# One decoder layer on one core: constant matmuls at the start, row scales by diagonals, two weight blocks kept, sums in two steps and on GpSimd, gmlp output stored whole

## The chip, the cores and the metric

The kernel runs on one core of one Trainium2 chip. The metric is the device time of one execution in microseconds (us), lower is better. Before the change it is 1546.96 us, the median of three runs (1548.9, 1546.96 and 1545.43). The engines are named as in the profile: PE (matmuls; PEld is its weight load), DVE (vector), ACT (scalar), POOL (GpSimd) and SP, whose queue issues most of the DMAs.

## The reference

One layer of a hybrid decoder on a prompt of 1024 tokens and on 64 sample tokens (8 sequences of 8) that share the weights; D = 1024, fp32 inputs.

```python
h = rmsnorm(x, norm_mix)
q, k, v, gu, gv, ga, gb = split_in(h @ w_in)     # 1024, 256, 256, 768, 768, 1024, 1024 columns
o, nk, nv = attn_prompt(q, k, v, sinks)          # window 128; the samples use a cache
vn = layernorm(jax.nn.gelu(gv), ln_g, ln_b)
s = spatial_gating(jax.nn.gelu(gu), vn, ws, bs)  # u * (W_s LN(v) + b) in chunks of 128
merged = jax.nn.sigmoid(ga) * (o @ w_pa) + jax.nn.sigmoid(gb) * (s @ w_pb)
x = x + merged @ w_out
f, nconv = conv_ffn(rmsnorm(x, norm_ffn), w_up, conv_w, conv_b, w_down, conv_prev)
return x + f, ...
```

`rmsnorm` is x / sqrt(mean(x²) + eps) times a gain. What the change touches is `h = rmsnorm(x, norm_mix)`, the product `h @ w_in`, and the way s gets from `spatial_gating` to `s @ w_pb`.

## The kernel before

**Precision.** Every operand of a matmul is split into a high part, which is the value rounded to fp32r, and a low part, which is the rest (`split`, L39 to L41: the ACT cast is L40, the DVE subtraction L41). One product then takes three matmuls: high·high, high·low, low·high.

**Groups and stages.** The tokens are in two groups: group 0 has 576 (64 samples and four blocks of 128), group 1 has 512 (four blocks of 128). The stages follow one another on PE, and what follows is about the first three:

- *Tokens* (to about 112 us). v has 256 columns, gv has three blocks of 256. The tokens are the stationary operand, the weights move (matmul line L489). A block of 256 weight columns is two items of 512 KB, each loaded to `wraw` and split into `w2h` and `w2l` (128x8x128 each time); there are two buffers of each. The order is v, gv0, gv1, gv2 for group 0 and the same again for group 1, so every block is loaded and split twice. v and gv come out as rows of tokens, so their scale 1/rms is one number for each partition (`rstg`).
- *Pairs* (about 112 to 475 us). q, k, gu and the two gates come out transposed. Here the weights are stationary (matmul line L288), and two weight tiles of 128 columns are taken together as a pair in a Strassen-Winograd scheme with seven products, `Chain.product`. It needs sums of the four quarters of a pair's weights (`Weights.total`, L173, four sums of 128x512 to `ws`, two buffers) and sums of the activations (`combine`, L250 to L253: two subtractions on POOL, then two steps on DVE that use them). A sum or a quarter is then split to `wh` and `wl`. The list of pairs begins with three *single* pairs that are done for group 0 only (FEWA = 3), then come 13 for both groups, then three singles for group 1 only.
- *Attention and branch* (from about 475 us) reads s and the queries back.

**The row scales.** `stats(g)` gets the sum of squares of the rows (`rs`, made by L562 on DVE), and from it 1/rms twice: one number for each partition by matmuls with a column of ones (L462), and as a full 128-row copy for the transposed activations, by matmuls of ones with `rs` (L467), two square roots on ACT and a reciprocal of the whole tile on DVE (L469). The jobs `t0_job` and `t1_job`, one for each step of the tokens stage, scale x by it (L603), call `combine`, and split the result for group 0 (`T0h`) or write it out for group 1 (`t1d`). It is read back and split (`t1_split`) during the first singles.

**Queues.** SP issues its DMAs in the program's order: weight items, x, the stores of gv (L521) and of the pairs' results. The weight stream is `Weights.get(ahead, loads)`: with each product it makes sure that the next operands are split and that `loads` more items are on their way, in a ring of four raw buffers. Each engine works its instructions in order, so an instruction that waits holds back those behind it.

**The gmlp output.** `mix_job` makes s for one channel group, splits it into high and low, and stores both planes (L743). `load_s` (L785) reads both planes back in the last singles and in the attention stage, straight to where PE uses them.

## Time and profile before

| what | value |
|---|---|
| runs | 1548.9, 1546.96, 1545.43 us, median 1546.96 |
| the profiled execution | 1547.57 us |
| span of its instructions | 1545.9 us (1.67 us of the execution lie around it) |
| mean granted PE clock | 0.993 |
| HBM read, written | 203.36 MB, 94.26 MB |
| DMA rate over the span | 193 GB/s |

The windows used below give for a stretch of time how long each engine was busy, with the number of its instructions in brackets, the granted PE clock as a share of full speed (PEclk), the busy share of the DMA engines and their rate. PE's busy time counts a matmul that runs at half clock as busy, so idle time and clock are read together.

### The profile page before, as it was taken

The page shows a single profiled execution, that of the slowest core. Times are in us where ns is not written, and L with a number is a line of the kernel's source. Part 1 is how long each engine was busy: PE and PEld are TensorE (multiplying, and loading weights), DVE is VectorE, ACT ScalarE, POOL GpSimd, SP SyncE. Part 2 cuts the span into 40 slices and gives each one's busy share as a digit, 9 for nine tenths or more (in the row PEclk, how much of TensorE's full clock was granted, in tenths as well). Part 3 has the DMA queues.
Part 4 walks back from the last instruction along what each step waited for, and adds up shares of the span by engine and source line. Part 5 has one row for each costly group of instructions (what it writes and reads, how often), then busy time and mean ns, then how long its engine had stood idle before and what let it go on. Part 6 is the DMA issues. An engine that isn't in the chain of part 4 may idle for free.

```text
span 1545.9 us, 30252 instructions
## 1 busy us (share of the span) xinstructions
PE 1518.0 (98%) x11588; PEld 1470.5 (95%) x11588; DVE 1182.7 (77%) x1908; ACT 863.9 (56%) x1800; POOL 274.4 (18%) x390
## 2 busy tenths in 40 slices
PE   8998999999999999999999999999999999999997
PEld 8998999999998888997988999999999999999997
DVE  6688776686664686888767888898899888785685
ACT  6656676765454574774443555555555556353462
POOL 0021000111020121230134222232232222000003
PEclk9999999999999999999999999999999999999999
DMA  6678344667779645828987423332233226973453
GB/s 230 226 259 297 136 161 177 223 193 244 262 271 325 230 164 179 265 81 300 329 304 265 159 90 112 120 125 99 101 141 114 79 93 219 360 246 94 122 176 131
DMA packets 134688, 297.63 MB, mean 193 GB/s; under 512 B 15504, under 2 KB 35792, under 8 KB 134544
## 3 DMA queue, kind: packets, MB, share of 16 engines
q1 hardware_dynamic: 134400, 295.69, 55.9%
q8 instruction: 91, 1.49, 0.4%
q14 instruction: 53, 0.43, 0.1%
q10 hardware_dynamic: 144, 0.01, 0.0%
HBM read 203.36 MB, written 94.26 MB: 193 GB/s over the span
## 4 chain that ended last, share of the span: by engine, by line
PE 78%; DVE 5%; DMA 3%; ACT 3%; issue 2%; POOL 1%; SPq 0%; POOLq 0%; ACTq 0%; DVEq 0%
PE st L288 45%; PE mm L234 15%; PE dn L1545 13%; PE po L1116 1%; PE sc L1068 1%; DMA sd<-sx 1%; DMA wraw<-wt 1%; PE pt L1095 1%; DVE wl L41 1%; ACT s L1085 1%; DVE ws L173 0%; DVE tl L41 0%; ACT wh L40 0%; DVE sx L41 0%; DVE s L1088 0%
## 5 line engine op out<-in xcount | busy, mean ns | idle before, releaser
L288 PE MATMUL st<-th,wh 128*128 128x256 f32 (+1 forms) x2128 | 613.9, 288 | 10.3 <-ACT ku L269 4.3
L288 PE MATMUL st<-tl,wh 128*128 128x256 f32 (+1 forms) x2128 | 610.9, 287 | 0.0
L288 PE MATMUL st<-th,wl 128*128 128x256 f32 (+1 forms) x2128 | 610.2, 287 | 0.0
L288 PEld LDWEIGHTS st<-th,wh 128*128 128x128 f32 x2128 | 402.3, 189 | 13.7 <-ACT k L269 6.1
L288 PEld LDWEIGHTS st<-th,wl 128*128 128x128 f32 x2128 | 402.6, 189 | 0.0
L288 PEld LDWEIGHTS st<-tl,wh 128*128 128x128 f32 x2128 | 402.2, 189 | 0.0
L40 ACT CAST wh<-wraw 128x512 fp32r<-128x512 f32 (+2 forms) x210 | 143.1, 692 | 105.0 <-PE mm L234 35.9
L41 DVE TENSOR_TENSOR wl<-wraw,wh 128x512 fp32r<-128x512 f32 (+2 forms) x210 | 163.0, 788 | 27.9 <-ACT wh L40 25.5
L1545 PE MATMUL dn<-tl,wh 128*128 128x288 f32 (+1 forms) x616 | 178.1, 289 | 0.2 <-DVE tl L41 0.2
L1545 PE MATMUL dn<-th,wh 128*128 128x288 f32 (+1 forms) x616 | 178.1, 289 | 0.0
L1545 PE MATMUL dn<-th,wl 128*128 128x288 f32 (+1 forms) x616 | 176.4, 286 | 0.0
L40 ACT CAST wh<-ws 128x512 fp32r<-128x512 f32 x168 | 103.0, 623 | 100.1 <-PE st L288 57.2
L41 DVE TENSOR_TENSOR wl<-ws,wh 128x512 fp32r<-128x512 f32 x168 | 116.4, 706 | 37.7 <-ACT wh L40 36.2
L1545 PEld LDWEIGHTS dn<-th,wh 128*128 128x128 f32 x616 | 116.9, 190 | 0.0
L1545 PEld LDWEIGHTS dn<-tl,wh 128*128 128x128 f32 x616 | 115.5, 187 | 0.5 <-DVE tl L41 0.5
L1545 PEld LDWEIGHTS dn<-th,wl 128*128 128x128 f32 x616 | 115.6, 188 | 0.0
L489 PE MATMUL st<-w2h,hh 128*128 128x256 f32 x288 | 82.5, 287 | 5.1 <-ACT w2h L40 5.1
L40 ACT CAST th<-traw 128x544 fp32r<-128x544 f32 (+1 forms) x85 | 54.4, 642 | 58.7 <-PE dn L1545 36.0
L276 POOL TENSOR_TENSOR z<-kn,k 128x288 f32<-128x288 f32 (+1 forms) x32 | 31.7, 995 | 289.6 <-ACT kn L271 286.0
L489 PE MATMUL st<-w2l,hh 128*128 128x256 f32 x288 | 82.0, 285 | 1.0 <-DVE w2l L41 1.0
L489 PE MATMUL st<-w2h,hl 128*128 128x256 f32 x288 | 81.7, 284 | 0.0
L41 DVE TENSOR_TENSOR tl<-traw,th 128x544 fp32r<-128x544 f32 (+1 forms) x85 | 61.5, 727 | 26.3 <-ACT th L40 26.1
(263 smaller groups left out, 2956.1 us busy)
## 6 DMA issues: line engine op xcount, KB each, us to landing
wraw<-wt SPq DMA_DIRECT2D x141, 512.0 KB
traw<-td SPq DMA_DIRECT2D x77, 272.0 KB
td<-za SPq DMA_DIRECT2D x22, 544.0 KB
wraw<-wt SPq DMA_DIRECT2D x35, 256.0 KB
upd<-hl SPq DMA_DIRECT2D x14, 512.0 KB
td<-t SPq DMA_DIRECT2D x11, 544.0 KB
qd<-q SPq DMA_DIRECT2D x8, 576.0 KB
q<-qd SPq DMA_DIRECT2D x8, 576.0 KB
```

What stands on the lines that cost most here:

```text
L40: S.copy(hi, src)
L41: V.tensor_sub(lo, src, hi.bitcast(F32))
L234: PE.matmul(ps[:, lo:lo + c1 - c0], u[:, k, :], v[:, c0:c1], start=(k == 0 and i == 0), stop=(k == nk - 1 and i == 2))
L276: op(to, pick(x, to, lo, hi), pick(y, to, lo, hi))
L288: PE.matmul(ps, u[:, kk, :], v, start=first and kk + i == 0, stop=kk == 3 and i == 2, skip_group_check=True)
L489: PE.matmul(ps, u[:, lo:lo + P], v[:, k, :], start=k + i == 0, stop=k == KD - 1 and i == 2)
L1068: PE.matmul(ps[:, h, o0:256], q, kst[kv][:, e, k0:cur + P], start=e == 0, stop=e == 1)
L1085: S.activation(s[:, h], s[:, h], AF.Exp, bias=nm[:, h:h + 1], accum_out=dn[:, h:h + 1])
L1095: PE.transpose(pt[:, h * P:h * P + P], s[:, h, 0:P], ident)
L1116: PE.matmul(po, v[:, kv, :], t, start=e == 0, stop=e == len(parts) - 1)
L1545: PE.matmul(place(m, e), u[:, m, :], v[:, lo:hi], start=new and i + k == 0 and (e == 0 or m % 2 == 0), stop=i == NU - 1 and k == 2, skip_g ...
```

## The change

1. **Constant matmuls.** Eight matmuls of a 128x128 tile of ones with itself are issued on PE ahead of the first real ones.
2. **Row scales by diagonals.** The full copy of 1/rms is made out of the one number for each partition: DVE multiplies the identity by it (a diagonal for each block of tokens), PE multiplies ones by the diagonal, ACT copies the result to `rs`. This is a job (`rows`) in the next block of the tokens stage. The matmuls of ones with `rs`, the four square roots on them and the two reciprocals of 576 and 512 columns are gone.
3. **Two blocks kept.** The order for group 0 is gv0, gv1, v, gv2. Group 1 then begins with v and gv2, whose weights still lie in the two buffers, and takes gv0 and gv1, loaded and split again. Four items of 512 KB, four casts and four subtractions are gone. The group's first steps have other jobs beside them than before.
4. **Sums in two steps.** `first_sums` scales x and issues the two POOL subtractions one job ahead of `sums_of`, which does the two DVE steps on them.
5. **Stores of gv** are issued from ACT's queue, and no longer from SP's.
6. **Single pairs.** The weight sums of the first pairs (14 sums of 128x512) are POOL's; the others stay on DVE. In most singles the last products of a pair load two items ahead, not one. The jobs that split T1 leave out every fourth product.
7. **gmlp unsplit.** s is stored as one plane, and read back to a stage buffer and split there (12 casts and 12 subtractions, in the last singles and ahead of the attention stage, where before there were 12 splits in the pairs stage).

The diff, cut to the lines that change:

```diff
         self.loaded = self.emitted = self.used = 0
-        self.sm = None
+        self.sm, self.adds = None, V
...
             t = self.sm.tile([P, 4, P], F32, name="ws", bufs=2)
-            V.tensor_add(t, x, y)
+            self.adds.tensor_add(t, x, y)
...
 t1d = [dr(f"t1d{kk}", [P, 7, 256]) for kk in range(4)]
-sd_ = [[dr(f"sd{g}{c}", [P, 2, n]) for c in range(NG)] for g, n in ((0, 576), (1, 512))]
+sd_ = [[dr(f"sd{g}{c}", [P, n]) for c in range(NG)] for g, n in ((0, 576), (1, 512))]
...
-    def dest256(key, half):
+    def dest256(key, half, again=False):
...
         def ready():
-            return "pool" in wide
+            return "pool" in wide and ("again" in wide or not again)
...
-    for g in range(2):
-        for i in range(2):
-            W.add(wt(V0 + i), KD, dest256(("v", g), i))
-        for i in range(6):
-            W.add(wt(GV0 + i), KD, dest256(("gv", g, i // 2), i % 2))
+    blocks = {"gv0": GV0, "gv1": GV0 + 2, "gv2": GV0 + 4, "v": V0}
+    for key in ("gv0", "gv1", "v", "gv2"), ("gv0", "gv1"):
+        for x in key:
+            for i in range(2):
+                W.add(wt(blocks[x] + i), KD, dest256(x, i, len(key) == 2))
...
-        acc, n2 = rsg[g], groups[g]["n"] // 2
+        acc, n = rsg[g], groups[g]["n"]
...
         V.reciprocal(rstg[g], rstg[g])
-        for h in range(2):
-            s, ps = slice(n2 * h, n2 * h + n2), bank()[:, :n2]
-            PE.matmul(ps, ones, acc[:, s], start=True, stop=True)
-            S.activation(acc[:, s], ps, AF.Sqrt, bias=eps, scale=1.0 / D)
-        V.reciprocal(acc, acc)
...
+        dg = stage(n)
+        for i, (name, lo) in enumerate(groups[g]["toks"]):
+            m = NS if name == "s" else P
+            V.tensor_scalar(dg[0:m, lo:lo + m], ident[0:m, 0:m], rstg[g][0:m, i:i + 1], None, ALU.mult)
...
+        def rows():
+            ps, at = None, 512
+            for name, lo in groups[g]["toks"]:
+                m = NS if name == "s" else P
+                if at + m > 512:
+                    ps, at, lo0 = bank(), 0, lo
+                PE.matmul(ps[:, at:at + m], ones[0:m], dg[0:m, lo:lo + m], start=True, stop=True)
+                at += m
+                if at + P > 512 or lo + m == n:
+                    S.copy(acc[:, lo0:lo + m], ps[:, :at])
+        return rows
...
         S.activation(v, ps, AF.Gelu_apprx_tanh, scale=rstg[g][:, i:i + 1])
-        nc.sync.dma_start(gvd[groups[g]["toks"][i][0]][:, 256 * p3:256 * p3 + 256], v)
...
-    def tokens(g, key, out, jobs):
-        W.get()
-        W.get()
+        nc.scalar.dma_start(gvd[groups[g]["toks"][i][0]][:, 256 * p3:256 * p3 + 256], v)
...
+    def tokens(g, key, out, jobs, new=True):
+        if new:
+            W.get()
+            W.get()
...
     xk = [hp0.tile([P, 576], F32, name=f"x{k}") for k in range(KD)]
-    places = [dest256(("v", 0), i)[1]() for i in range(2)]
+    places = [dest256("gv0", i)[1]() for i in range(2)]
...
             nc.sync.dma_start(xk[0][:, 320:576], a["xt"][0:P, 320:576])
+    ps = bank()
+    for _ in range(8):
+        PE.matmul(ps[:, 0:P], ones, ones, start=True, stop=True)
...
             for i, (_, lo) in enumerate(toks0):
-                mm_tok(ps5[i], 0, lo, wide["v", 0], kx)
+                mm_tok(ps5[i], 0, lo, wide["gv0"], kx)
...
         load_late()
-    stats(0)
+    rows = stats(0)
...
     for i in range(len(toks0)):
-        v_out(0, i, ps5[i])
+        gv_out(0, i, 0, ps5[i])
...
-    jobs = [x_job(k) for k in range(KD)]
-    for p3 in range(3):
-        tokens(0, ("gv", 0, p3), lambda i, ps: gv_out(0, i, p3, ps), jobs)
+    jobs = [rows, *(x_job(k) for k in range(KD))]
+    tokens(0, "gv1", lambda i, ps: gv_out(0, i, 1, ps), jobs)
+    tokens(0, "v", lambda i, ps: v_out(0, i, ps), jobs)
+    tokens(0, "gv2", lambda i, ps: gv_out(0, i, 2, ps), jobs)
...
     hs0o.close()
-    stats(1)
+    rows = stats(1)
...
+    half = {}
...
+    def first_sums(n):
+        def go():
+            g, kk = n // 4, n % 4
+            x_in(n + 1)
+            n2, x = groups[g]["n"] // 2, xin.pop(n)
+            for e in range(2):
+                k = kk + 4 * e
+                V.scalar_tensor_tensor(x[:, e], x[:, e], gains[:, 0, k:k + 1], rsg[g], ALU.mult, ALU.mult)
+            t4 = xr.tile([P, 4, 288], F32, name="t", bufs=2)[:, :, :n2]
+            b11, b12, b21, b22 = (x[:, e, n2 * h:n2 * h + n2] for e in range(2) for h in range(2))
+            G.tensor_sub(t4[:, 2], b22, b12)
+            G.tensor_sub(t4[:, 0], b11, b12)
+            half[n] = x, t4, b11, b21
+        return go
...
     def sums_of(g, kk):
-        x_in(4 * g + kk + 1)
-        n2, x = groups[g]["n"] // 2, xin.pop(4 * g + kk)
-        for e in range(2):
-            k = kk + 4 * e
-            V.scalar_tensor_tensor(x[:, e], x[:, e], gains[:, 0, k:k + 1], rsg[g], ALU.mult, ALU.mult)
-        t4 = xr.tile([P, 4, 288], F32, name="t", bufs=2)[:, :, :n2]
-        combine(t4, *(x[:, e, n2 * h:n2 * h + n2] for e in range(2) for h in range(2)))
-        return x[:, 0, 0:n2], t4, x[:, 1].rearrange("p (h c) -> p h c", h=2)
+        x, t4, b11, b21 = half.pop(4 * g + kk)
+        V.scalar_tensor_tensor(t4[:, 1], t4[:, 2], -1.0, b11, ALU.mult, ALU.subtract)
+        V.scalar_tensor_tensor(t4[:, 3], t4[:, 1], -1.0, b21, ALU.mult, ALU.subtract)
+        return b11, t4, x[:, 1].rearrange("p (h c) -> p h c", h=2)
...
     none = lambda: None
-    jobs = [lambda: x_in(0)] + [x for kk in range(4) for x in (t0_job(kk), none)] + [t1_job(kk) for kk in range(4)]
-    tokens(1, ("v", 1), lambda i, ps: v_out(1, i, ps), jobs)
-    for p3 in range(3):
-        tokens(1, ("gv", 1, p3), lambda i, ps: gv_out(1, i, p3, ps), jobs)
...
+    def both(*gos):
+        return lambda: [go() for go in gos]
...
+    jobs = [both(rows, lambda: x_in(0)), first_sums(0)]
+    for n in range(4):
+        jobs += [both(t0_job(n), first_sums(n + 1))] + [none] * (n % 2 == 0)
+    jobs += [both(t1_job(n), first_sums(n + 5)) for n in range(3)] + [t1_job(3)]
+    tokens(1, "v", lambda i, ps: v_out(1, i, ps), jobs, False)
+    wide["again"] = True
+    W.emit(W.used + 2)
+    tokens(1, "gv2", lambda i, ps: gv_out(1, i, 2, ps), jobs, False)
+    for p3 in range(2):
+        tokens(1, f"gv{p3}", lambda i, ps: gv_out(1, i, p3, ps), jobs)
...
             V.tensor_mul(t[:, soff:n], t[:, soff:n], gu[:, soff:n])
-            sx = mp.tile([P, 2, 576], F32R, name="sx")[:, :, :n]
-            split(sx[:, 0], sx[:, 1], t)
-            nc.sync.dma_start(sd_[g][c], sx.bitcast(F32))
+            nc.sync.dma_start(sd_[g][c], t)
...
     def load_s(g, pool, c):
-        x = pool.tile([P, 2, groups[g]["n"]], F32R, name=f"s{g}{c}")
-        nc.sync.dma_start(x.bitcast(F32), sd_[g][c])
+        n = groups[g]["n"]
+        raw, x = stage(n), pool.tile([P, 2, n], F32R, name=f"s{g}{c}")
+        nc.sync.dma_start(raw, sd_[g][c])
+        split(x[:, 0], x[:, 1], raw)
...
         for j in range(7):
-            w = W.get(3, 4 if at == len(seq) - 1 and j > 3 else 1)
+            W.adds = G if at < FEWA else V
+            single = at < FEWA - 1 or at >= len(seq) - FEWA - 1
+            w = W.get(3, 4 if at == len(seq) - 1 and j > 3 else 2 if single and j > 4 else 1)
...
                 done.pop(0)()
-            if jobs and 7 * at + j > 2:
+            if jobs and 7 * at + j > 2 and (at >= FEWA or (7 * at + j) % 4 < 3):
...
```

What it moves, first on POOL, from the last subtractions for group 0 to the first products of the pairs. `t` are the activations' sums, `ws` the weights' sums, `z` the pairs' results. Before:

```order
L251 TENSOR_TENSOR t_1563<-x_1517 128x256
L250 TENSOR_TENSOR t_1604<-x_1558 128x256
L251 TENSOR_TENSOR t_1604<-x_1558 128x256
L250 TENSOR_TENSOR t_1654<-x_1599 128x256
L251 TENSOR_TENSOR t_1654<-x_1599 128x256
L276 TENSOR_TENSOR z10_1771<-kn_1875,k5_1820 128x288
```

After:

```order
L173 TENSOR_TENSOR ws_1804<-wraw_1464,wraw_1466 128x512
L628 TENSOR_TENSOR t_1549<-x_1503 128x256
L627 TENSOR_TENSOR t_1549<-x_1503 128x256
L173 TENSOR_TENSOR ws_1881<-wraw_1625 128x512
L173 TENSOR_TENSOR ws_1903<-ws_1881,wraw_1623 128x512
L628 TENSOR_TENSOR t_1587<-x_1544 128x256
L627 TENSOR_TENSOR t_1587<-x_1544 128x256
L173 TENSOR_TENSOR ws_1928<-ws_1903,wraw_1623 128x512
L173 TENSOR_TENSOR ws_1951<-wraw_1623,wraw_1625 128x512
L173 TENSOR_TENSOR ws_2038<-wraw_1629 128x512
L276 TENSOR_TENSOR z10_1772<-kn_1870,k5_1821 128x288
```

Between the subtractions for group 1 now stand sums of weights: in all, six of the 14 stand ahead of the last of these subtractions, eight behind it.

On DVE at the first statistics (`rst` is the number for each partition, `rs` the full copy, `vst` and `gv` the outputs of the first block). Before:

```order
L562 TENSOR_TENSOR rs_231<-rs_231,x_257 128x576
L562 TENSOR_TENSOR rs_231<-rs_231,x_258 128x576
L376 COPY_PREDICATED c_wss<-stg 64x384
L464 RECIPROCAL rst_233<-rst_233 128x5
L41 TENSOR_TENSOR w2l<-wraw,w2h 128x8x128
L469 RECIPROCAL rs_231<-rs_231 128x576
L41 TENSOR_TENSOR vst<-gv,vst 128x4x64 x2
L507 TENSOR_TENSOR gv<-gv 128x256
```

After:

```order
L578 TENSOR_TENSOR rs_231<-rs_231,x_257 128x576
L578 TENSOR_TENSOR rs_231<-rs_231,x_258 128x576
L41 TENSOR_TENSOR w2l<-wraw,w2h 128x8x128
L376 COPY_PREDICATED c_wss<-stg 64x384
L464 RECIPROCAL rst_233<-rst_233 128x5
L469 TENSOR_SCALAR stg<-c_ident,rst_233 64x64
L469 TENSOR_SCALAR stg<-c_ident,rst_233 128x128 x4
L41 TENSOR_TENSOR w2l<-wraw,w2h 128x8x128
L45 SCALAR_TENSOR_TENSOR hl_608<-stg,c_gains,hh_607 128x512
L624 SCALAR_TENSOR_TENSOR x<-x,c_gains,rs_231 128x576
```

The reciprocal of 576 columns is gone, and five products with the identity stand in its place; the vst splits follow later, since the first block is now gv0.

On SP's queue in the last singles (`sd` is the stored s, `wraw` the raw weights of the last pairs). Before:

```order
L801 DMA msamp<-msamp 128x384
L814 DMA ckt<-ckt 128x1024
L785 DMA s_6016<-sd_175 128x1152
L785 DMA s_6038<-sd_176 128x1152
L144 DMA wraw<-wt 128x1024
L778 DMA sg0d_129<-z_5885 128x512
```

After:

```order
L824 DMA stg<-sd_175 128x576
L144 DMA wraw<-wt 128x1024
L781 DMA sd_186<-stg 128x512
L816 DMA sg0d_136<-z_5560 128x576
L816 DMA sg0d_136<-z_5562 128x512
L816 DMA sg1d_144<-z_5563 128x512
L841 DMA kn<-ksn 128x128
L841 DMA vs<-vsd 64x256
L841 DMA msamp<-msamp 128x384
L816 DMA sg1d_144<-z_5561 128x576
L854 DMA ckt<-ckt 128x1024
L144 DMA wraw<-wt 128x1024
```

Ahead of the weights stood two loads of s with two planes (128x1152). Now there is one load with one plane (128x576), and the next load of s stands behind the last weight item of these rows.

## The prediction

> **What bounds the kernel now.** I read the page first, then the windows, then the waits, the chain and the timeline of the stretches that stand out.
>
> ```profile
> span 1545.9 us, 30252 instructions
> PE 1518.0 (98%) x11588; PEld 1470.5 (95%) x11588; DVE 1182.7 (77%) x1908; ACT 863.9 (56%) x1800; POOL 274.4 (18%) x390
> ```
>
> PE is busy for 98% of the span, so matmuls set the time, and a change that leaves their number alone can win only where PE stands or runs at half clock. That is 27.9 us idle in the whole program plus the half-clock stretches. The windows show where these lie in the part that the change touches.
>
> ```profile
> 0.00:23.00 23.00, 17.23 (x123) 17.02 (x123) 17.23 (x29) 17.14 (x28) 0.20 (x4) 1.00 0.83 278
> 23.00:28.00 5.00, 4.90 (x24) 4.08 (x24) 2.80 (x4) 4.40 (x11) 0.00 (x0) 0.66 0.09 20
> 28.00:70.00 42.00, 42.00 (x360) 42.00 (x358) 27.98 (x39) 24.61 (x45) 3.70 (x4) 1.00 0.76 259
> 100.00:112.00 12.00, 11.01 (x97) 10.81 (x96) 11.37 (x16) 3.28 (x7) 3.81 (x4) 1.00 0.72 243
> 112.00:140.00 28.00, 22.87 (x160) 21.94 (x159) 21.27 (x38) 15.63 (x33) 5.42 (x5) 0.94 0.87 292
> 145.00:160.00 15.00, 15.00 (x112) 14.53 (x111) 14.96 (x26) 11.79 (x24) 0.86 (x1) 1.00 0.64 225
> 160.00:440.00 280.00, 280.00 (x2277) 279.80 (x2276) 201.06 (x341) 175.68 (x345) 27.32 (x29) 1.00 0.59 203
> 440.00:455.00 15.00, 14.62 (x129) 14.42 (x128) 8.10 (x13) 9.86 (x21) 7.99 (x18) 1.00 0.94 335
> 455.00:465.00 10.00, 6.95 (x35) 6.75 (x35) 7.02 (x11) 4.07 (x8) 0.90 (x1) 0.66 0.57 220
> 465.00:475.00 10.00, 10.00 (x91) 10.00 (x89) 3.77 (x6) 5.61 (x12) 1.14 (x1) 1.00 0.89 300
> ```
>
> The long middle (160 to 440) is full at full clock: nothing is to be had there. Four places lose time: the start; the end of the tokens stage (1.0 us of idle PE in 100 to 112); the first singles (5.1 us idle in 112 to 140, and PEclk 0.94, which is 28 × 0.06 × 2 = 3.4 us at half clock); and the last singles (0.4 and 3.05 us idle, and PEclk 0.66 in 455 to 465). In the last, 35 matmuls are done in 10 us where the next window does 91, so they are worth 35 × 10/91 = 3.8 us and 6.2 us are lost; with 129 × 10/91 = 14.2 us, 440 to 455 loses another 0.8. What PE waits for, in 100 to 140 and then in 440 to 475:
>
> ```profile
> ACT wh L40 <- DVE ws L173: 16.7, 6, 8.1
> POOL t L250 <- DVE x L603: 12.6, 2, 6.4
> PE st L288 <- ACT k L269: 3.3, 3, 1.4
> PE st L288 <- ACT kn L271: 1.8, 1, 1.8
> PE st L489 <- DVE w2l L41: 1.0, 1, 1.0
> ...
> ACT wh L40 <- DVE ws L173: 4.2, 3, 3.6
> DVE ws L173 <- DMA wraw<-wt: 3.4, 1, 3.4
> PE st L288 <- ACT ku L269: 3.0, 1, 3.0
> ```
>
> The page names the evictions k, kn and ku of ACT as PE's releasers. ACT is only 15.63 of 28 us busy, and it stood 16.7 us in its order ahead of `wh` casts for weight sums that DVE (21.27 of 28 us) had not made; the evictions queue behind these casts. So the first singles are late by DVE's sums, and the last by one weight transfer:
>
> ```profile
> 444.66 0.91 SPq L785 DMA_DIRECT2D s<-sd  x2
> 445.66 0.38 SPq L144 DMA_DIRECT2D wraw<-wt  x1
> ...
> 445.66 10.29 DMA wraw<-wt
> ```
>
> It took 10.29 us from its issue, behind two loads of s of 576 KB (the row is in the next part's fence).
>
> **The change part by part.** The prices:
>
> ```profile
> L41 DVE TENSOR_TENSOR w2l<-wraw,w2h 128x1024 fp32r<-128x1024 f32 x13 | 15.6, 1213 | 1.2 <-ACT w2h L40 1.2
> L173 DVE TENSOR_TENSOR ws<-wraw 128x512 f32<-128x512 f32 x8 | 6.6, 826 | 0.0
> L173 DVE TENSOR_TENSOR ws<-ws,wraw 128x512 f32<-128x512 f32 x8 | 6.1, 764 | 0.2
> L1239 POOL TENSOR_TENSOR nacc<-nacc,stg 128x512 f32<-128x512 f32 x6 | 10.2, 1694 | 21.9 <-ACT stg L1238 21.9
> 95.42 3.13 POOL L250 TENSOR_TENSOR t<-x 128x288 f32<-128x288 f32 x1 [2.74 <-DVE x L603]
> 98.50 0.81 POOL L251 TENSOR_TENSOR t<-x 128x288 f32<-128x288 f32 x1
> s<-sd SPq DMA_DIRECT2D x6, 576.0 KB
> 5.11 0.80 PE L489 MATMUL st<-w2h,hh 128*128 128x256 f32 x2 [5.11 <-ACT w2h L40]
> 10.43 0.41 PE L489 MATMUL st<-w2h,hh 128*128 128x256 f32 x1
> 10.79 0.28 PE L489 MATMUL st<-w2h,hl 128*128 128x256 f32 x1
> 21.02 1.61 DVE L562 TENSOR_TENSOR rs<-rs,x 128x576 f32<-128x576 f32 x2
> 22.69 1.27 PE L462 MATMUL st<-c_ones,rs 128*128 128x1 f32 x10 [0.67 <-DVE rs L562]
> 26.64 3.75 DVE L469 RECIPROCAL rs<-rs 128x576 f32<-128x576 f32 x1 [0.62 <-ACT rs L468]
> ```
>
> *Constant matmuls: 0.* PE stands until 5.11 anyway. Eight matmuls of 128 columns, fp32 and not fp32r, are not in the trace. The first two of 256 columns took 0.80 us; at that price each, eight end by 4.3 us, from about 1.1; at twice it, by 7.5. I take the first. With the clock up earlier (the matmuls take 0.41 us until 10.6 and 0.28 after), the first block would end sooner, but the statistics at 22.69 waited 0.67 us for DVE's `rs` sums, not for PE. The bounds are +2.4 (they end late, nothing hides it) and, if DVE too could run earlier, a gain: that is a rival.
>
> *Diagonals: 0.* PE's work is nearly the same (four matmuls of 288 and 256 columns against nine of up to 128). DVE loses 3.75 us and its like for group 1, and gets nine small products with the identity; a 128-column one is less than a quarter of the 512 that cost 0.83, so about 2 us in all. DVE had room there (27.98 of 42 us), so neither sets the end. The first block now needs ACT's Gelu at its eviction, behind which PE's banks wait: 24 matmuls in 23 to 28 are its cover. Without it, a microsecond either way.
>
> *Two blocks kept: −1.0.* Four casts, four w2l at 1.213 us and 2 MB of loads are gone, 4.9 us of DVE, where it was busy 11.37 of 12 us. The wait of 1.0 us for w2l at 100 to 112 was of this work; at least one of the two blocks split again is earlier. Bounds: 0 and −1.3.
>
> *Stores of gv on ACT: 0.* 27 issues near the 0.38 us of SP's issue are 10 us over 80 us, and ACT was busy 24.61 of 42. Its cover is that room; without it each would delay an eviction by 0.4 us.
>
> *First singles: −4.8.* I count what the rows show as lost: the waits of 3.3 and 1.8, and half of the 3.4 us at half clock, 6.8 in all. (The 160 matmuls at the 15/112 us of the next window are 21.4 of 28 us, which agrees.) DVE gives up 14 sums at about 0.8 (11 us), the 4.9 us above, and the two reciprocals; scaling and POOL's subtractions start a job earlier, for which POOL waited 12.6. On POOL a 128x512 sum took 1.69 us where it added two tiles. Six of the 14 stand ahead of group 1's last subtraction, the other eight take 13.5 us of the 33.8 us that the three singles last (252 matmuls at 15/112 us). That is slack, if the price holds. I leave 2 us, because a chain of three sums now takes 5.1 us and not 2.4, DVE is still needed for every split, and DMA at 0.87 stays. Bounds: +1 (a chain late once) and −7.8.
>
> By the Trainium skill (SBUF — State Buffer, section "SBUF: two separate sides") DVE and GpSimd share a port pair that one holds for a whole instruction while the other blocks, DVE with two SBUF inputs included. The trace has one sign of it, the 3.13 us subtraction above beside the 0.81 us of the next one. By this rule POOL's 1.69 us sums would also hold up DVE's splits, and the part would give nearly nothing.
>
> *Last singles: −4.5.* 6.2 + 0.8 = 7.0 us were lost. Of s, 1152 KB stood ahead of the late weights, and now 288 KB: 864 KB at the 335 GB/s of 440 to 455 are 2.6 us. Weight loads are also issued two ahead at the end of each pair, so this one is issued earlier. The wait of 3.0 us then nearly goes, and with it the pause that stands ahead of the half clock. Bounds: −2.6 (the bytes alone) and −7.0. I take 4.5.
>
> *Splits of s: +1.* Twelve casts and twelve subtractions move from the middle, which was full of matmuls and hid them, to the last singles and the turn to the attention stage, at about 0.6 us each on ACT and 0.7 on DVE. In 455 to 475 both have room (10.79 of 20 us on DVE), but a cast in ACT's order waits for its load, and evictions wait behind it. Bounds: 0 and +4.
>
> The sum is −1.0 − 4.8 − 4.5 + 1.0 = −9.3 on the profiled execution of 1547.57 us: 1538.3. The median of the runs is 0.6 below that execution, so the forecast is 1538.
>
> **The rivals.**
>
> *POOL's sums become the path of the singles (slower).* For it: the 3.13 us for 288 columns, which for 512 would be 5.6 us. Eight sums at 5.6 are 44.8 us against 33.8 us of PE work: 11.0 lost and the 4.8 of the first singles not won. With −1.0 − 4.5 + 1.0 that is +6.5, 1554. It decides from 4.2 us a sum. Against it: six sums of the same shape at a mean of 1.69.
>
> *Casts of s hold up ACT's evictions at the turn.* DMA is at 0.94 in 440 to 455, so s may come late, and six casts stand among the last pairs' evictions. At +4 in place of +1, and with only the 2.6 of bytes won: −1.0 − 4.8 − 2.6 + 4 = −4.4, 1542.5.
>
> *The first singles stay late for another reason* (T1 comes late behind POOL's sums, or DMA is the limit): −1.0 − 4.5 + 1.0 = −4.5, 1542.5.
>
> *The start gains too.* If the constant matmuls raise the clock early, the stretch from 5.1 to 10.6 takes half: PE would be 2.7 us ahead, and 1535 comes out if it lasts. Against it stands the 0.67 us wait for `rs`. The Trainium skill (TensorE: Matmul & The Clock Gate, section "What's actually happening") has the clock rise after a busy window of some 3.4 us, by which the eight would earn this; no run yet shows them.
>
> *The waits only move.* DVE is 14.96 of 15 us busy right after the first singles, so work put off from 112 to 140 is done there, and nothing is won: 1546.
>
> **How the numbers follow.** Changes under 0.2% (3.1 us) can't be told from none. I give the forecast 0.55, the POOL rival 0.12, the two of 1542.5 together 0.19, the start 0.06, no net change 0.08. Faster gets 0.55, 0.06 and 0.19 in full: 0.80. Same gets 0.08, slower 0.12. The likeliest one's own range is 1533 to 1543. The range for all goes from 1531 (every part at its better bound, −16) to 1547, which leaves out the POOL rival and some of the best cases.
>
> **What would show it.** Right: no wait of L489 for w2l before the first pair; in the first singles idle PE under 3 us and PEclk at 1.00, with POOL's L173 rows near 1.7 us; the last pairs' `wraw` landing in under 8 us and no half-clock stretch around 460; the statistics still at about 22.7 us. Wrong: L173 on POOL at over 4 us, DVE's splits stretched beside it, a wait of PE for `wh` or `wl` in the first singles; waits of ACT for stage buffers loaded from `sd`, with PE behind, at 455 to 480; a first double pair that waits for T1's splits.

## The result and the profile after

The changed kernel takes 1556.13 us (median of 5, 1553.26 to 1560.99) where the kernel before takes 1546.41 (median of 5). The ratio is 1.0077, with a 95% interval of 1.0058 to 1.0096: slower by 0.6 to 1%. The profiled execution is the slowest of the five, 1560.99 us, so its stages are read for where the time goes, and the sizes come from the ratios.

The page's first lines and the windows of the changed kernel (columns as before: length, then busy time of PE, PEld, DVE, ACT and POOL, PEclk, DMA share, GB/s):

```profile
span 1559.2 us, 30332 instructions
PE 1519.9 (97%) x11614; PEld 1470.4 (94%) x11614; DVE 1174.6 (75%) x1897; ACT 863.9 (55%) x1795; POOL 294.0 (19%) x404
...
0.00:23.00 23.00, 19.29 (x140) 18.28 (x141) 17.47 (x29) 18.25 (x29) 0.20 (x4) 1.00 0.86 284
...
100.00:112.00 12.00, 11.73 (x102) 11.53 (x102) 10.67 (x14) 4.66 (x10) 5.47 (x5) 1.00 0.61 198
112.00:140.00 28.00, 18.45 (x121) 17.86 (x120) 16.02 (x21) 10.26 (x23) 12.43 (x10) 0.82 0.74 244
140.00:160.00 20.00, 16.26 (x112) 15.51 (x111) 18.60 (x24) 15.94 (x31) 9.33 (x7) 0.95 0.74 232
...
455.00:475.00 20.00, 16.86 (x146) 16.46 (x146) 16.78 (x28) 13.65 (x29) 6.68 (x13) 1.00 0.87 301
475.00:520.00 45.00, 42.48 (x343) 35.71 (x342) 25.19 (x57) 20.48 (x49) 1.09 (x2) 0.96 0.82 265
```

In the first singles PE does 121 matmuls in 112 to 140 where it did 160, at a PEclk of 0.82 where it had 0.94, and 140 to 160, which was full (the row of the kernel before is below), now has 3.7 us idle. ACT and DVE are less busy there than before (10.26 and 16.02 of 28 us, against 15.63 and 21.27), so neither is short of capacity: they wait.

```profile
140.00:160.00 20.00, 20.00 (x150) 19.53 (x149) 19.96 (x34) 16.46 (x34) 1.75 (x2) 1.00 0.69 233
```

From the first L288 matmul to the first one that needs both groups the three singles last 52.4 us (114.8 to 167.2) and lasted 41.7 (115.7 to 157.4). That is 10.7 us more, about what the medians differ by (9.7); the tokens stage ends 0.9 us earlier. What waits in 100 to 165 us (a selection; who, for whom: us in total, times, longest):

```profile
POOL ws L173 <- DVE wl L41: 17.1, 5, 9.1
PE st L288 <- ACT k L269: 12.0, 4, 5.5
ACT wh L40 <- POOL ws L173: 8.9, 5, 5.5
ACT th L40 <- DMA stg<-t1d: 6.3, 3, 5.3
PE st L288 <- ACT kn L271: 1.3, 1, 1.3
PE st L501 <- DVE w2l L41: 0.3, 1, 0.3
```

PE waits 13.6 us where it waited 6.1. The w2l wait is nearly gone, as forecast. The `wh` casts now wait for POOL's sums in place of DVE's, and POOL waits for DVE's splits. The two long waits of PE, in its timeline, with what ACT did up to them:

```profile
123.66 0.61 PE L288 MATMUL st<-th,wh 128*128 128x288 f32 x1 [5.51 <-ACT k L269]
...
130.96 0.61 PE L288 MATMUL st<-th,wh 128*128 128x288 f32 x1 [4.04 <-ACT k L269]
...
119.14 0.33 ACTq L533 DMA_DIRECT2D gvd<-gv  x1
119.57 0.47 ACT L532 ACTIVATE gv<-st,rst 128x256 f32<-128x256 f32 x1 [3.03 <-DMA x<-xt]
122.79 0.33 ACTq L533 DMA_DIRECT2D gvd<-gv  x1
123.21 0.40 ACT L269 COPY k<-st 128x288 f32<-128x288 f32 x1 [3.16 <-DMA wraw<-wt]
...
130.20 0.41 ACT L40 CAST th<-stg 128x256 fp32r<-128x256 f32 x1 [5.28 <-DMA stg<-t1d]
```

Ahead of the first, ACT had finished the last gv at 120.04 and issued its store only at 122.79; the eviction k stands behind that issue. A completion semaphore is how a DMA tells that it has landed. In this trace the program's 865 DMAs share eight of them, each taken 108 or 109 times, and the wait just ahead of each of these stores is for the semaphore that the store itself then takes: it waits for the DMA that had it last. Here that was a load of x (at 119.14) and a load of weights (at 122.79), with which gv has nothing to do. Ahead of the second, a cast of T1 (the activation sums of group 1) waits for its readback. Both are waits in ACT's order with PE's evictions behind them.

### The profile page after: what moved, and what is told of

It reads as the page before. It is cut to its first block, busy times and chain, and to the rows that moved or that the text cites. A ratio compares the mean times of both kernels' runs of the same rounds, so it can differ in the third digit from the quotient of the medians.

```text
span 1559.2 us, 30332 instructions
## 1 busy us (share of the span) xinstructions
PE 1519.9 (97%) x11614; PEld 1470.4 (94%) x11614; DVE 1174.6 (75%) x1897; ACT 863.9 (55%) x1795; POOL 294.0 (19%) x404
## 4 chain that ended last, share of the span: by engine, by line
PE 76%; DMA 7%; DVE 6%; ACT 4%; issue 3%; POOL 2%; SPq 1%; POOLq 0%; DVEq 0%; ACTq 0%
PE st L288 42%; PE mm L234 15%; PE dn L1587 11%; PE st L501 3%; DMA wraw<-wt 2%; PE po L1158 2%; PE sc L1110 1%; DMA stg<-sd 1%; DMA x<-xt 1%; DVE wl L41 1%; DVE tl L41 1%; DMA vnd<-v 1%; DMA v<-gvd 1%; PE pt L1137 1%; DMA stg<-t1d 1%
## 5 line engine op out<-in xcount | busy, mean ns | idle before, releaser
L288 PE MATMUL st<-th,wh 128*128 128x256 f32 (+1 forms) x2128 | 613.8, 288 | 21.2 <-ACT k L269 15.7
L288 PE MATMUL st<-tl,wh 128*128 128x256 f32 (+1 forms) x2128 | 610.4, 287 | 0.0
L288 PE MATMUL st<-th,wl 128*128 128x256 f32 (+1 forms) x2128 | 609.9, 287 | 0.0
L288 PEld LDWEIGHTS st<-th,wh 128*128 128x128 f32 x2128 | 401.9, 189 | 25.4 <-ACT k L269 18.3
L288 PEld LDWEIGHTS st<-th,wl 128*128 128x128 f32 x2128 | 402.0, 189 | 0.0
L288 PEld LDWEIGHTS st<-tl,wh 128*128 128x128 f32 x2128 | 401.5, 189 | 0.0
L41 DVE TENSOR_TENSOR wl<-wraw,wh 128x512 fp32r<-128x512 f32 (+2 forms) x210 | 166.4, 804 | 32.4 <-ACT wh L40 30.0
L1587 PEld LDWEIGHTS dn<-th,wh 128*128 128x128 f32 x616 | 115.7, 188 | 4.0 <-DVE x L1597 3.5
L1587 PEld LDWEIGHTS dn<-th,wl 128*128 128x128 f32 x616 | 115.7, 188 | 0.0
```

Source lines behind the costliest of these rows:

```text
L41: V.tensor_sub(lo, src, hi.bitcast(F32))
L288: PE.matmul(ps, u[:, kk, :], v, start=first and kk + i == 0, stop=kk == 3 and i == 2, skip_group_check=True)
L1587: PE.matmul(place(m, e), u[:, m, :], v[:, lo:hi], start=new and i + k == 0 and (e == 0 or m % 2 == 0), stop=i == NU - 1 and k == 2, skip_g ...
```

## The experiments

All ratios are to the kernel before, run on the same chip in the same rounds, with 95% intervals. Changed kernels are compared with one another by these ratios.

| kernel | ratio | interval |
|---|---|---|
| the change | 1.0077 | 1.0058 to 1.0096 |
| gv stores on SP | 1.0076 | 1.0061 to 1.0090 |
| weight sums on DVE | 1.0041 | 1.0024 to 1.0059 |
| both (stores on SP, weight sums on DVE) | 1.0007 | 0.9993 to 1.0020 |
| gmlp split as before | 1.0090 | 1.0076 to 1.0104 |
| before, gv stores on ACT | 1.0010 | 0.9996 to 1.0024 |
| before, weight sums on POOL | 1.0085 | 1.0065 to 1.0106 |
| both, and activation sums in one step | 0.9985 | 0.9971 to 0.9998 |
| both, and all blocks reloaded | 1.0025 | 1.0013 to 1.0037 |
| before, POOL for weight sums only | 1.0035 | 1.0021 to 1.0049 |
| before, subtractions on DVE | 0.9962 | 0.9945 to 0.9979 |
| the kernel of 0.9985, without constant matmuls | 0.9992 | 0.9978 to 1.0006 |
| before, two items ahead | 0.9998 | 0.9983 to 1.0013 |
| the change, all sums on DVE | 1.0009 | 0.9996 to 1.0022 |
| the kernel of 0.9985, with subtractions on DVE | 0.9984 | 0.9971 to 0.9996 |
| the change, all sums on DVE, stores on SP | 0.9977 | 0.9965 to 0.9988 |

An edit to one line also moves others in this kernel's engine orders, so that a ratio holds for the edit with what it moves.

**Stores, weight sums, both.** The two theories on the two long waits.

```diff
-nc.scalar.dma_start(gvd[groups[g]["toks"][i][0]][...], v)
+nc.sync.dma_start(gvd[groups[g]["toks"][i][0]][...], v)
```

> The changed kernel with the gv stores back on SP's queue. Theory A: in the changed kernel a store on ACT's queue waits for an earlier, unrelated DMA (the trace shows 2.75 us between a finished gv and the issue of its store at 122.79 us) and holds up the eviction of the first pair, for which PE waits 5.5 us. Then that wait is gone here, PE's waits in 100 to 165 us fall from 13.6 us to about 8, and the ratio to before falls from 1.0077 to about 1.004. Rival B: POOL's weight sums are what ACT and PE wait for. Then the wait stays at some place of the first singles and the ratio stays at 1.007 to 1.008.

```diff
-W.adds = G if at < FEWA else V
+W.adds = V
```

> The changed kernel with all weight sums on DVE again. Theory A (stores on ACT): the first wait of 5.5 us stays, ratio 1.006 to 1.008. Rival B (POOL's sums of 1.5 to 1.7 us, in chains with the splits, set the first singles): PE's waits in 100 to 165 us fall from 13.6 us to 5 or less, the ratio is 1.002 or lower.

> The changed kernel with the gv stores on SP's queue and all weight sums on DVE. If A and B each hold for one of the two long waits (5.5 us at 118 and 4.0 us at 126), they add up: PE's waits in 100 to 165 us are under 5 us and the ratio is 0.999 to 1.001. If the second wait comes from the T1 sums in two steps (x loaded late), some 4 us of it stay with either and the ratio is about 1.003.

The stores alone gave nothing (1.0076). The weight sums alone gave 0.0036, less than the 0.0057 or more that theory B had, and the two together 0.0070. So they stand beside one another: with the stores moved, the wait came at the same place behind other things. In that run the second pair's raw weights were issued at 117.77, right behind a store of T1 sums (116.80) that waited for DVE and POOL, and a `wh` cast on ACT waited 9.4 us for them. With both undone the first singles last 44.0 us, still over the 41.7 of before.

**gmlp split again.** The diff is part 7 of the change, undone.

> The changed kernel with s stored as two planes again, split when it is made. Theory C: the smaller s saved at the last singles what its splits cost at the turn to the attention stage (PE lost 12.9 us in 440 to 520 before, 13.1 us after), so the ratio stays within 0.001 of 1.0077. Rival D: loading weights two ahead alone mends the last singles and the splits at the turn only cost; then the loss in 440 to 520 falls to 8 us or less and the ratio to 1.004 or lower.

1.0090 against 1.0077, intervals that overlap: neither theory D's gain nor a loss that can be told.

**One part alone on the kernel before.**

```diff
-nc.sync.dma_start(gvd[groups[g]["toks"][i][0]][...], v)
+nc.scalar.dma_start(gvd[groups[g]["toks"][i][0]][...], v)
```

> The kernel before with one part alone: the gv stores go out from ACT's queue. Theory A (a store in ACT's order waits for an earlier unrelated DMA, and evictions queue behind it): PE's waits for k, kn and ku in the first singles grow from 5.1 us to 8 to 11, or the tokens stage ends later by as much; ratio 1.002 to 1.004. Rival: the stores are harmless where POOL has no sums; ratio 1.000 within 0.001.

```diff
-V.tensor_add(t, x, y)
+self.adds.tensor_add(t, x, y)
...
 for j in range(7):
+    W.adds = G if at < FEWA else V
```

> The kernel before with one part alone: the weight sums of the first pairs on POOL. Theory B (a POOL sum takes 1.3 to 1.8 us in place of 0.7, and the chain sum, cast, split, next sum with two buffers is on PE's path): the first singles last 48 us or more in place of 41.7, ratio 1.004 to 1.006. Rival: POOL's sums hurt only beside the rest of the change (later T1, stores on ACT); ratio within 0.001 of 1.000.

The stores alone come to 1.0010, which this measurement can't tell from nothing. POOL's 14 sums alone cost 0.85%, 13 us: as much as the whole change, and more than theory B had. The first singles last 52.2 us there. In this kernel's trace, first POOL and then DVE around the end of the tokens stage (start, duration):

```profile
114.59 1.34 POOL L173 TENSOR_TENSOR ws<-ws,wraw 128x512 f32<-128x512 f32 x1 [0.69 <-DVE wl L41]
116.63 1.34 POOL L173 TENSOR_TENSOR ws<-wraw 128x512 f32<-128x512 f32 x1 [0.70 <-DVE wl L41]
...
114.71 1.78 DVE L41 TENSOR_TENSOR wl<-ws,wh 128x512 fp32r<-128x512 f32 x1
116.74 1.78 DVE L41 TENSOR_TENSOR wl<-ws,wh 128x512 fp32r<-128x512 f32 x1
118.44 0.68 DVE L41 TENSOR_TENSOR wl<-wraw,wh 128x512 fp32r<-128x512 f32 x1
...
L41 DVE TENSOR_TENSOR wl<-ws,wh 128x512 fp32r<-128x512 f32 x14 | 16.4, 1178 | 1.9 <-ACT wh L40 1.8
```

A split that starts just after a POOL sum takes 1.78 us, and one that starts while POOL is idle 0.68. The sum ends at 114.59 + 1.34 = 115.93, and the split at 116.49, 0.56 after it: DVE stood while POOL worked, and then did its own work. The last line sums up 90 to 170 us: the splits of sums have a mean of 1178 ns. This is the rule of the Trainium skill that the prediction weighed (SBUF — State Buffer, "SBUF: two separate sides"), and the trace agrees. The other half of the price is in the waits of the same kernel, 100 to 170 us (the first, second, third and PE's longest):

```profile
ACT wh L40 <- POOL ws L173: 23.9, 8, 11.1
POOL ws L173 <- DVE wl L41: 16.0, 8, 9.1
POOL t L250 <- DVE x L603: 11.5, 3, 7.0
PE st L288 <- ACT kn L271: 9.3, 2, 9.1
```

The 9.1 us wait of PE is a queue: a weight sum stood on POOL behind two subtractions for T1 (132.77), which waited 7.0 us for their x. The queue is on DVE too: the split that this sum then waited for stood in DVE's order behind the scaling of the same x, which had waited 5.26 us for a store of T1. That left two mechanisms to part, the queue and the port.

**The queue or the port.** POOL for weight sums only, with its control.

```diff
-def combine(t4, b11, b12, b21, b22):
+def combine(t4, b11, b12, b21, b22, T=G):
-    G.tensor_sub(t4[:, 0], b11, b12)
-    G.tensor_sub(t4[:, 2], b22, b12)
+    T.tensor_sub(t4[:, 0], b11, b12)
+    T.tensor_sub(t4[:, 2], b22, b12)
...
-combine(t4, *(x[:, e, n2 * h:n2 * h + n2] for e in range(2) for h in range(2)))
+combine(t4, *(x[:, e, n2 * h:n2 * h + n2] for e in range(2) for h in range(2)), T=V)
```

> The kernel before with the weight sums of the first pairs on POOL (that alone was 1.0085), and the activation sums of the tokens stage wholly on DVE, so that POOL has nothing but weight sums there. Theory Q (queue: the sums of weights stand in POOL's order behind subtractions for T1 whose x comes late; PE waited 9.1 us for that): the long waits are gone, the ratio falls to within 0.002 of the control with DVE's subtractions alone. Theory P (port: a DVE split beside a POOL sum takes 1.78 us in place of 0.68, and each link of the chain is longer): the ratio stays 0.005 or more above the control, and DVE's wl splits of sums keep a mean over 1.0 us.

> Control for the run on POOL with weight sums only: the kernel before with the activation sums of the tokens stage wholly on DVE and nothing on POOL there. 16 subtractions of 288 or 256 columns at about 0.45 us are 7 us more on a DVE that is nearly full at 100 to 112 and 140 to 160 us; against it the waits of DVE for POOL's subtractions (3.3 us) go. Ratio 0.999 to 1.004 with either theory.

The queue on POOL is not the main cost: without subtractions on POOL its sums still cost 1.0035 − 0.9962 = 0.0073, most of the 0.0085. One sign of theory Q came true, since no wait of PE is over 3.8 us there, but the ratio isn't near the control's. Of theory P's signs one was weaker than expected, since the splits of sums have a mean of 816 ns and not over 1000; but a sum is 1.7 us there, where DVE took 0.7 to 0.8. This trace is of the fastest of that kernel's ten executions (1542.55 us, median 1548.84), so it shows less than the usual loss. First POOL's weight sums, then the control's:

```profile
L41 DVE TENSOR_TENSOR wl<-ws,wh 128x512 fp32r<-128x512 f32 x16 | 12.7, 816 | 3.8 <-ACT wh L40 3.6
L173 POOL TENSOR_TENSOR ws<-ws,wraw 128x512 f32<-128x512 f32 x7 | 11.9, 1702 | 22.8 <-DVE wl L41 20.7 <-issue 1.3 <-POOL ws L173 0.7
```

```profile
L41 DVE TENSOR_TENSOR wl<-ws,wh 128x512 fp32r<-128x512 f32 x19 | 12.9, 685 | 1.5 <-ACT wh L40 1.4
L173 DVE TENSOR_TENSOR ws<-ws,wraw 128x512 f32<-128x512 f32 x10 | 8.1, 805 | 0.2
```

POOL is idle 20.7 us ahead of its sums, waiting for DVE's splits, because a sum needs one of two `ws` buffers and each is free only when cast and split are done. So a sum, a cast, a split and the next sum are one chain over three engines, in which POOL's busy time says nothing of its slack. How much of the 0.0073 is the longer sum and how much the held split was not parted. An estimate from the trace of the 1.0085 kernel bounds the second: from 92 us to the end of the first singles, 13 splits of 128x512 took over 0.8 us, and each of them ended 0.55 us after a POOL instruction, 11 times a weight sum. Together they took 20.8 us where 13 at 0.68 are 8.8, so DVE stood for some 12 us. The 14 sums that it gave up are 9.8 us at 0.7. So DVE got nothing back for them.

The control itself was the surprise. It gives DVE 16 subtractions more and is the fastest kernel of the study, 0.9962: the first singles last 39.5 us in place of 41.7. One thing that went away is a wait. In the kernel before, from 90 to 165 us, DVE stands 3.3 + 2.9 = 6.2 us for POOL's subtractions, ahead of the steps that use them:

```profile
L252 DVE SCALAR_TENSOR_TENSOR t<-t,x 128x256 f32<-128x256 f32 x4 | 2.2, 552 | 3.3 <-POOL t L251 3.3
L252 DVE SCALAR_TENSOR_TENSOR t<-t,x 128x288 f32<-128x288 f32 x2 | 0.9, 458 | 2.9 <-POOL t L251 2.9
```

The control has no such wait. That this is what makes it faster was not tested by itself.

**Steps and blocks.** On the kernel with stores on SP and weight sums on DVE (1.0007). In the first edit `sums_of` and the job list are those of before; the second is this:

```diff
-for key in ("gv0", "gv1", "v", "gv2"), ("gv0", "gv1"):
+for key in ("gv0", "gv1", "v", "gv2"), ("v", "gv2", "gv0", "gv1"):
...
-tokens(1, "v", lambda i, ps: v_out(1, i, ps), jobs, False)
+tokens(1, "v", lambda i, ps: v_out(1, i, ps), jobs)
```

> The changed kernel with gv stores on SP and all weight sums on DVE (that was 1.0007), and also the activation sums in one step again. Theory T (the two steps hold x's two buffers a job longer, so the loads of x, T1's sums and, behind T1's stores on SP, the second pair's weights come late): the first singles fall from 44.0 us to 42 or less, ratio 0.998 to 0.9995. Rival: the lateness has another cause; singles 43 to 46 us, ratio 1.000 to 1.002.

> The changed kernel with gv stores on SP and all weight sums on DVE (1.0007), and also all four blocks loaded and split again for group 1, in the changed order. If keeping two blocks helps (the tokens stage ends 3.3 us earlier than before, 112.4 for 115.7 us): the stage ends at 114 us or later, ratio 1.001 to 1.003. Rival: the two kept blocks hold both buffers, so that the others are split late and the raw ring is free late; then the pairs' weights come earlier here, first singles 42 us or less, ratio 0.998 to 1.000.

The two steps cost 0.0022 here, and the singles fall from 44.0 to 39.5 us (114.7 to 154.2). Keeping the blocks is worth 0.0018, 2.8 us, by the medians. Both differences are near the limit of what can be told: the intervals (0.9971 to 0.9998, 0.9993 to 1.0020, 1.0013 to 1.0037) just overlap.

**Constant matmuls, and two items ahead.**

```diff
-for _ in range(8):
-    PE.matmul(ps[:, 0:P], ones, ones, start=True, stop=True)
```

> The version that beat the kernel before (gv stores on SP, all weight sums on DVE, activation sums in one step: 0.9985) without the eight constant matmuls. If they are worth nothing, because DVE's sums of squares and not PE end last ahead of the statistics: ratio 0.998 to 0.999. Rival (the clock comes up early and the start is 2.7 us shorter with them): ratio 1.000 to 1.0005.

```diff
-w = W.get(3, 4 if at == len(seq) - 1 and j > 3 else 1)
+w = W.get(3, 4 if at == len(seq) - 1 and j > 3 else 2 if at >= len(seq) - FEWA - 1 and j > 4 else 1)
```

> The kernel before with one edit alone: in the last singles two weight items are loaded ahead at the end of a pair, not one. If the late weights of the last pair were an issue that came late, the last singles fall from 35.4 us to 31 or less and the ratio is 0.997 to 0.998. If it was the bytes of s in front of them, the last singles stay over 34 us and the ratio is within 0.001 of 1.

Neither moves the time by what can be told. In the second, both expectations failed: the last singles do fall, from 35.4 to 29.4 us, and the median doesn't. The other kernels tell why. Those with the code of before in this part have last singles of 29.5 us (gv stores on ACT), 30.1 (POOL sums), 31.1 and 31.7 (the queue test and its control), counted from the stage's first matmul to its last; only the one profiled execution of before has 35.4. In the kernel with the POOL sums the same late transfer took 8.25 us and not 10.29, and PE waited 0.8 us and not 3.0. So the stall that the forecast mended was, as far as these traces tell, for the most part that of one execution.

**All sums on DVE.** To see what is left of the change without POOL.

```diff
-G.tensor_sub(t4[:, 2], b22, b12)
-G.tensor_sub(t4[:, 0], b11, b12)
+V.tensor_sub(t4[:, 2], b22, b12)
+V.tensor_sub(t4[:, 0], b11, b12)
```

> The changed kernel with every sum of the tokens stage and of the first pairs on DVE, weights and activations; gv stores stay on ACT's queue and the two steps stay. If POOL beside DVE was the whole cost and the forecast was right about the rest: the ratio is 0.994 to 0.997, as low as the kernel before with DVE's subtractions (0.9962) or lower. If the stores on ACT and the later T1 cost for themselves: 1.000 to 1.004, near the run with DVE's weight sums alone (1.0041).

> As the changed kernel with every sum on DVE, but with the gv stores on SP's queue. If a store on ACT costs for itself (its wait for an unrelated DMA): 0.002 or more below the same kernel with the stores on ACT. If it was only the other side of POOL's late sums: within 0.001 of it.

> The best version of the change so far (gv stores on SP, weight sums on DVE, activation sums in one step: 0.9985) with the activation sums' subtractions on DVE too. If taking POOL out is worth the same as on the kernel before (-0.0038) and adds to the rest: 0.9940 to 0.9955. If the two cover the same waits of the first singles: 0.996 to 0.9985.

The ladder from the change down is 1.0077, weight sums off POOL 1.0041, subtractions off POOL 1.0009, stores off ACT 0.9977: three steps of 0.0036, 0.0032 and 0.0032, some 5 us each. So POOL was not the whole cost: the first expectation above fails, and the stores cost for themselves in the changed kernel once the weight sums are off POOL. With the subtractions still on POOL the price was the same, 0.0034 (1.0041 to 1.0007). On the kernel before they came to 0.0010, so that their price may hang on something else in the change; that was not tested. The two steps cost nothing that shows without POOL: they have 0.9977 there and the one step 0.9984. On top of one step POOL's removal adds nothing in the changed kernel (0.9985 and 0.9984), though it gave 0.0038 on the kernel before.

## Why the prediction was wrong

The forecast was 1538 us, and 1556 came out. The rival "POOL's sums become the path of the singles", with 1554, named the place and the size, but its condition was not met. That its number is near is luck: it takes eight sums at 5.6 us, and they took 1.5 to 1.7.

**First singles, −4.8: the step that failed.** It read: "the other eight take 13.5 us of the 33.8 us that the three singles last. That is slack, if the price holds." The price held: no weight sum took over 2.3 us. In the changed kernel, 20 to 170 us:

```profile
L173 POOL TENSOR_TENSOR ws<-ws,wraw 128x512 f32<-128x512 f32 x7 | 12.2, 1737 | 14.0 <-DVE wl L41 13.9
L173 POOL TENSOR_TENSOR ws<-wraw 128x512 f32<-128x512 f32 x7 | 10.3, 1468 | 9.3 <-DMA gvd<-gv 3.8 <-DVE wl L41 3.2 <-DVE tl L41 1.2
```

At 1.47 to 1.74 us, far from the 4.2 from which the rival was to decide, the sums cost 13 us on the kernel before. The 33.8 us were PE's work alone; the stage lasts 41.7 us in the trace of before. Set against 41.7 the slack would have looked larger still. (The window 145 to 160, which the rival "The waits only move" calls right after the first singles, lies for the most part within them.) Busy time against stage time is a test of throughput; here a chain of four operations with two buffers stands ahead of ACT's evictions, and DVE is held while POOL works. The prediction had named splits of DVE stretched beside POOL as a sign of being wrong, and this sign came: in the changed kernel four splits of 128x512 take 1.77 or 1.78 us. The same step took the late sums as a sign that DVE had too much to do. The control shows otherwise: with 16 subtractions more on DVE and POOL out of the way the stage is 2.2 us shorter. In the trace of before DVE waits for POOL's subtractions, and a DVE instruction that is held beside POOL is counted as busy by the page.

**The rule of the Trainium skill** on the shared ports was put in a sentence beside the sum, with "nearly nothing" for the gain of the part. The measured case was worse than that, a loss of 13 us on the kernel before. DVE stood for about as long as it was relieved, as the rule has it, and a sum took 1.5 us or more in place of 0.7 besides.

**Stores on ACT, 0.** It weighed only the 0.38 us of an issue. What it left out is the wait ahead of the issue, for an unrelated DMA. The price is 0.0032 to 0.0034 in the changed kernel once the weight sums are off POOL, and nothing that shows beside them (1.0077 and 1.0076).

**Sums in two steps** were booked as a gain within the first singles ("start a job earlier"). They cost 0.0022 with POOL's subtractions, and nothing that can be told without.

**Two blocks kept, −1.0:** right in sign by the medians, which give 2.8 us.

**Constant matmuls, 0:** the rows agree. They end at 4.68 us, where the estimate had 4.3. The clock rises at 5.6 us and not at 10.7, as the rival on the start had it, and the statistics still start when DVE's sums are there, at 22.56 (before, 22.69), with PE waiting 1.45 us in place of 0.67:

```profile
1.15 3.53 PE L563 MATMUL st<-c_ones 128*128 128x128 f32 x16 [1.15 <-DVE c_ones L73]
5.67 0.28 PE L501 MATMUL st<-w2h,hl 128*128 128x256 f32 x1
22.56 0.61 PE L462 MATMUL st<-c_ones,rs 128*128 128x1 f32 x4 [1.45 <-DVE rs L578]
```

The runs with and without them can't be told apart.

**Last singles, −4.5:** mis-sized, since the 7 us of loss were read from one execution in which one transfer was late; the traces of four other kernels with the same code had 4 to 6 us less there. The changed kernel's last singles take 33.9 us against the 35.4 of that execution, and so more than in those four. **Splits of s, +1:** the chain of the changed kernel in 440 to 490 us has the loads of s that the casts wait for, 6 to 7.4 us from issue to landing:

```profile
455.44 7.38 DMA stg<-sd
466.28 5.95 DMA stg<-sd
477.37 6.12 DMA stg<-sd
```

Neither part shows by itself: with s split as before the changed kernel has 1.0090 in place of 1.0077, and two items ahead on the kernel before 0.9998. The diagonals were not tried alone.

**A place without a term.** From the first matmul for both groups to the last singles the changed kernel takes 284.8 us, and the kernel before 282.2. The six traces with the code of before have 282.2 to 282.9 there, the eleven with the change's 282.7 to 285.0. The cause stays open.

The best version found is the kernel before with the tokens stage's subtractions on DVE, 0.9962 (0.9945 to 0.9979), without any part of the change. The best one with parts of the change is 0.9977.

## What to carry to other kernels

An idle engine is not slack for a link in a chain: price a moved operation by what each link waits for (its duration, its buffers, the evictions queued behind it), and add what it holds up on the engine that it shares ports with. Ahead of work moved to a second engine, try the opposite: on the kernel before, taking the work that is there away from POOL was worth more than any offload here. A stall seen in one profiled execution should be found in a second one before its removal is counted.

## What was not expected of the hardware

A DVE split of 128x512 took 1.78 us beside a POOL sum and 0.68 alone, and ended 0.56 us after the sum: DVE waited for the rest of the POOL instruction. The regularity is striking: of the 13 stretched splits in that trace, every one ended 0.55 us after the POOL instruction beside it. The DVE instruction counts as busy all the while.

The 3.13 us subtraction on POOL in the first profile, next to one of 0.81, looks like the other side of it, POOL held by DVE. These are DVE's rows beside it:

```profile
94.47 1.54 DVE L603 SCALAR_TENSOR_TENSOR x<-x,c_gains,rs 128x576 f32<-128x576 f32 x2
95.93 0.69 DVE L41 TENSOR_TENSOR wl<-wraw,wh 128x512 fp32r<-128x512 f32 x1
96.53 1.35 DVE L41 TENSOR_TENSOR tl<-t,th 128x1152 fp32r<-128x1152 f32 x1
```

DVE works without a gap to 96.53 + 1.35 = 97.88, and the subtraction ends at 95.42 + 3.13 = 98.55, 0.67 after it. In the kernel with POOL's sums one of 3.12 us ends 0.66 after such a run of DVE. If so, POOL stood behind three DVE instructions in a row, and not one. No run tests this by itself.
